# One decoder step on one core: order of the recurrence's last chunks, and where the output weights lie in memory

## The chip, the cores and the metric

The kernel runs on one NeuronCore of a Trainium2 chip. The metric is the device time of one execution in microseconds (us), taken as the median of several runs. The engines are TensorE (PE; its weight loads are listed apart as PEld), VectorE (DVE), ScalarE (ACT), GpSimd (POOL) and SyncE (SP, which here only issues DMAs). DMAs are issued by SP and by POOL; each of the two has one queue of its own, which it works through in order.

## The reference

One inference step of a two-layer decoder in float32, for a prompt of 16 + 1024 rows and eight samples of 8 rows each. Layer one is an mLSTM with 8 heads (key width 64, value width 128); layer two is an attention layer. Each is followed by a SwiGLU network. The part that matters here, for one layer-one chunk:

```python
s = jnp.einsum('bhtk,bhsk->bhts', q, k) * jnp.exp(dmat - m_t[..., None])
num = w_inter[..., None] * jnp.einsum('bhtk,bhkv->bhtv', q, C) + jnp.einsum('bhts,bhsv->bhtv', s, v)
h = num / jnp.maximum(jnp.abs(den), jnp.exp(-m_t))[..., None]
C_new = w_c[..., None, None] * C + jnp.einsum('bhs,bhsk,bhsv->bhkv', w_g, k, v)
...
h = rmsnorm(h.transpose(0, 2, 1, 3), mh_g)
out = (h.reshape(B, T, HV).astype(xn.dtype) * jax.nn.sigmoid(og)) @ w_out
```

The outputs are the rows of both groups, the new states, and the keys and values.

## The kernel before

Activations lie with the model dimension on the partitions (8 blocks of 128) and the 1104 rows (80 sample and meta rows, 1024 prompt rows) along the free dimension. A product in nearly full precision is made of three matmuls: each operand is split into a high part (a copy that rounds to the matmul's type, on ACT) and a low part (the difference, by a subtraction), and high x high, low x high and high x low are added up in PSUM (`mm3`, lines 206 to 208).

`recurrence` goes through nine chunks: chunk 0 of 80 rows, chunks 1 to 8 of 128. For a chunk, `chunk_load` fetches queries and keys (qk), decay rows (eb) and query weights (wb) through POOL's queue; `chunk_decay` makes eight DVE operations on eb and ACT takes its exponential; `chunk_scores` multiplies keys by queries (PE, sps) and the result by eb (DVE); `chunk_keys` prepares kw and wb (DVE); `chunk_state` makes the new state C (PE cp, DVE, then POOL multiplies C by the chunk's decay); `chunk_out` makes the outputs in two halves z = 0 and 1, each from a carried product (PE nps from C and wb) and an intra-chunk product (PE nps from vA and eb), which DVE (den) and ACT (vA) take out of PSUM. All of this is written out by hand in program order (`manual_schedule` for PE, DVE, ACT and POOL), a chunk ahead where it can be.

Between these steps PE gets other work by the calls `f(n)` and `g(n)`. Up to chunk 6 both issue n slices of the output gate's projection (mmA, 24 matmuls a tile): ACT takes a finished tile out with a sigmoid (stg, line 994) and POOL stores it in memory (ogD). Three chunks make a group of rows; once a group is done, `norm_heads` normalises it in two steps: five small DVE operations and a square root on ACT (fA, line 1606), then, from DVE, the three multiplications of vA. For chunks 7 and 8 `g` issues gated heads instead, one a call whatever n is: `gate_head` transposes a head on PE into a PSUM bank (ghps, line 1628), multiplies it by gain and gate values on DVE (line 1629) in the place that holds these values (ogqk, ogeb), and splits it into xh (ACT, line 284) and xl (DVE, line 285). mmA and ghps share two PSUM banks. A place is filled again by a DMA through POOL's queue (line 1010). Ten heads are gated within the recurrence and fourteen later.

Then `mlp` starts with the output projection: units of 24 matmuls (pops), one per column group t (0 to 3, 276 rows each) and weight block m (0 to 7), each added to the hidden rows H by DVE. Its weights wait in memory, split already, as eight pairs of 1.05 MB (woD); SP loads them at line 547. Pairs 0 to 3 go to four tiles of a new pool (wo) that takes over memory of the recurrence, pairs 4 to 7 to slots that the recurrence's last tiles free. A load waits until what lay at its place is finished.

## Time and profile before

| | us |
|---|---|
| median of 3 runs | 2790.65 (2790.15 to 2793.41) |
| profiled execution, whole | 2792.57 |
| profiled execution, span | 2790.8 |
| PE busy | 2730.0 (98%) |
| DVE busy | 1786.6 (64%) |
| ACT busy | 1167.3 (42%) |
| POOL busy | 847.1 (30%) |

The recurrence ends and the output units begin near 410 us of the span. In rows of the profile a name such as `ghps<-ident,vA` is output and inputs by the program's tile names; L1628 is line 1628 of the kernel; a bracket at the end of a row gives the idle time of that engine before the instruction and what ended it. Rows with several instructions (x8) are merged, and their time is the sum.

### The profile page before, as it was taken

The numbers are of one execution on the slowest core, as the hardware profiler recorded it, in microseconds if no ns is written. First come the engines' busy times: TensorE is split into PE (matmuls) and PEld (weight loads), VectorE is DVE, ScalarE is ACT, GpSimd is POOL, SyncE is SP. The second block draws the span as 40 slices with busy tenths as digits, with TensorE's granted clock in tenths as the row PEclk, the third lists the DMA queues.
The fourth block names the chain that finished last, engine by engine and source line by source line (L and its number), as shares of the span: only waits on it lengthen the run. The fifth ranks groups of instructions, "written<-read, shape, count | busy, mean of one in ns | idle before, by whom it ended". The sixth has DMA issues, their size and how long they took to land. (4 is left out here: it accounts for less than half of the span.)

```text
span 2790.8 us, 60492 instructions
## 1 busy us (share of the span) xinstructions
PE 2730.0 (98%) x23525; PEld 2637.2 (94%) x23525; DVE 1786.6 (64%) x4008; ACT 1167.3 (42%) x2291; POOL 847.1 (30%) x1305
## 2 busy tenths in 40 slices
PE   9999989999999999999999999999999999999998
PEld 8999979999999999999999998777999999999998
DVE  5633556888887665573455444777388888765656
ACT  5432552423322333443444555777343223323345
POOL 3142333132322332124353202454313223323211
PEclk9999999999999999999999999999999999999999
DMA  7667556355554375544553786443524555526556
GB/s 213 178 182 180 153 153 207 100 151 167 166 174 146 114 240 177 194 148 153 187 178 129 239 292 201 162 138 95 150 82 132 177 176 167 163 91 229 185 193 222
DMA packets 432466, 473.06 MB, mean 170 GB/s; under 512 B 37015, under 2 KB 358291, under 8 KB 431155
## 3 DMA queue, kind: packets, MB, share of 16 engines
q1 hardware_dynamic: 380690, 320.25, 37.6%
q0 software_dynamic: 44848, 142.74, 15.6%
q10 hardware_dynamic: 6640, 6.21, 0.7%
q8 instruction: 185, 3.03, 0.4%
q14 instruction: 103, 0.84, 0.1%
HBM read 322.24 MB, written 146.83 MB: 168 GB/s over the span
## 5 line engine op out<-in xcount | busy, mean ns | idle before, releaser
L1685 PE MATMUL m<-xh,slot 128*128 128x276 f32 (+1 forms) x2752 | 538.9, 289 | 1.8 <-ACT fs L1714 1.8
L1685 PEld LDWEIGHTS m<-xh,slot 128*128 128x128 f32 x2752 | 439.0, 188 | 4.2 <-ACT fs L1714 2.4
L1685 PE MATMUL m<-xl,slot 128*128 128x276 f32 (+1 forms) x1376 | 396.7, 288 | 0.0
L1685 PEld LDWEIGHTS m<-xl,slot 128*128 128x128 f32 x1376 | 259.0, 188 | 0.0
L206 PE MATMUL tmps<-slot,xh 128*128 128x256 f32 (+2 forms) x864 | 243.2, 281 | 0.0
L208 PE MATMUL tmps<-slot,xl 128*128 128x256 f32 (+2 forms) x864 | 240.6, 278 | 0.0
L207 PE MATMUL tmps<-slot,xh 128*128 128x256 f32 (+2 forms) x864 | 240.6, 278 | 0.0
L285 DVE TENSOR_TENSOR slot<-slot,slot 128x1024 fp32r<-128x1024 f32 x124 | 162.0, 1307 | 60.7 <-ACT slot L284 59.2
L284 ACT CAST slot<-slot 128x1024 fp32r<-128x1024 f32 x124 | 129.4, 1044 | 143.2 <-PE m L1685 109.4
L207 PEld LDWEIGHTS tmps<-slot,xh 128*128 128x128 f32 (+1 forms) x864 | 159.2, 184 | 0.1
L206 PEld LDWEIGHTS tmps<-slot,xh 128*128 128x128 f32 (+1 forms) x864 | 158.4, 183 | 0.3
L208 PEld LDWEIGHTS tmps<-slot,xl 128*128 128x128 f32 (+1 forms) x864 | 158.6, 184 | 0.0
L206 PE MATMUL mmA<-xh,whi 128*128 128x384 f32 (+1 forms) x384 | 134.2, 349 | 3.1 <-ACT stg L994 3.0
L207 PE MATMUL mmA<-xl,whi 128*128 128x384 f32 (+1 forms) x384 | 128.1, 334 | 0.0
L208 PE MATMUL mmA<-xh,wlo 128*128 128x384 f32 (+1 forms) x384 | 128.0, 333 | 0.0
L285 DVE TENSOR_TENSOR slot<-vA,slot 128x1024 fp32r<-128x1024 f32 (+1 forms) x59 | 82.2, 1396 | 32.7 <-ACT slot L284 31.5
L285 DVE TENSOR_TENSOR slot<-Ht,slot 128x1024 fp32r<-128x1024 f32 (+1 forms) x59 | 82.1, 1395 | 32.7 <-ACT slot L284 31.5
L284 ACT CAST slot<-vA 128x1024 fp32r<-128x1024 f32 (+1 forms) x59 | 60.8, 1035 | 95.5 <-PE m L1685 90.5
L1789 DVE TENSOR_TENSOR ws<-ws 128x128 f32<-128x128 f32 x264 | 94.7, 359 | 8.9
L284 ACT CAST slot<-Ht 128x1024 fp32r<-128x1024 f32 (+1 forms) x59 | 60.7, 1034 | 94.6 <-PE m L1685 84.1
L2919 ACT ACTIVATE s<-s,nb 128x272 f32<-128x272 f32 (+7 forms) x126 | 98.9, 787 | 0.0
L2954 ACT COPY th<-tp 128x768 f32<-128x768 f32 (+1 forms) x80 | 73.5, 921 | 56.0 <-PE tp L2946 32.2
(793 smaller groups left out, 8631.7 us busy)
## 6 DMA issues: line engine op xcount, KB each, us to landing
ws<-in_w_down SPq DMA_DIRECT2D x176, 128.0 KB, 2.7
sD<-ws SPq DMA_DIRECT2D x176, 128.0 KB, 2.1
slot<-sD SPq DMA_DIRECT2D x40, 512.0 KB, 4.2
slot<-in_w_gate_up SPq DMA_DIRECT2D x36, 512.0 KB, 4.1
kp<-in_cache_k SPq DMA_DIRECT2D x32, 512.0 KB, 5.3
vp<-in_cache_v SPq DMA_DIRECT2D x32, 512.0 KB, 7.3
vA<-in_w_gate_up SPq DMA_DIRECT2D x26, 512.0 KB, 4.0
Ht<-in_w_gate_up SPq DMA_DIRECT2D x26, 512.0 KB, 4.0
```

The source lines that it names most:

```text
L206: mm(ps, sh, mh, start=first, stop=False)
L207: mm(ps, sh, ml, start=False, stop=False)
L208: mm(ps, sl, mh, start=False, stop=last)
L284: self.nc.scalar.copy(hi, src)
L285: self.nc.vector.tensor_tensor(out=lo, in0=src, in1=hi.bitcast(F32), op=ALU.subtract)
L1685: nc.tensor.matmul(u.ps[h, b], w[p][:, k], x[q][:, k], start=first and k == i == 0, stop=k == 3 and i == 2, skip_group_check=True)
L1789: tt(out=o, in0=a, in1=b, op=ALU.subtract)
L2919: nc.scalar.activation(ss[z, u], ss[z, u], AF.Exp, bias=nb[:, z : z + 1], accum_out=sm[:, u, z : z + 1])
L2954: nc.scalar.copy(th.rearrange("p x z (u h q) -> p h (x z u) q", h=2, q=64)[:, :, :n], pt[:, :, :n])
```

## The change

Five edits, none of which changes what is computed:

- **norm first.** Behind a chunk's first half, norm's first step is issued ahead of the eight decay operations.
- **loads half a chunk sooner.** The loads for chunk i + 3, which stood at the start of chunk i + 1, are issued right behind chunk i's second half.
- **heads one at a place.** In chunks 7 and 8 the five heads stand at five places: ahead of the state, behind it, behind the first half, within the second half, and behind it, instead of three and two in a row.
- **xl on POOL.** The ten heads within the recurrence subtract xl on POOL instead of DVE. The fourteen later ones keep DVE.
- **output weights.** The wo pool is shifted by a pad of 768 bytes a partition, and pairs 1 and 2 take other tiles of it. Pair 3 is loaded twice: a first copy into a tile of its own (wo3), which unit (0, 3) reads, and a second one behind pairs 4 to 7 into the pool's lowest tile, which column groups 1 to 3 read. The tile pool TA is opened after column group 0 instead of before.

On DVE, in chunk 6 (rd and fA are norm's small steps, eb the decay operations, den and vA the copies and the normalised rows). Before:

```order
L1419 TENSOR_TENSOR wb_4487<-qk_4485,wb_4487 128x512
L1381 SCALAR_TENSOR_TENSOR eb_4486<-eb_4486,tmA,cap 128x128 x8
L1601 SCALAR_TENSOR_TENSOR rd_4562<-den 128x24
L1602 TENSOR_TENSOR rd_4562<-rd_4562,tmA 128x24
L1603 RECIPROCAL rd_4562<-rd_4562 128x24
L1604 TENSOR_TENSOR fA_4563<-ssqA,rd_4562 128x24
L1605 TENSOR_TENSOR fA_4563<-fA_4563,rd_4562 128x24
L1608 RECIPROCAL fA_4563<-fA_4563 128x24
```

And of the change:

```order
L1442 TENSOR_TENSOR wb_4299<-qk_4298,wb_4299 128x512
L1628 SCALAR_TENSOR_TENSOR rd_4554<-den 128x24
L1629 TENSOR_TENSOR rd_4554<-rd_4554,tmA 128x24
L1630 RECIPROCAL rd_4554<-rd_4554 128x24
L1631 TENSOR_TENSOR fA_4555<-ssqA,rd_4554 128x24
L1632 TENSOR_TENSOR fA_4555<-fA_4555,rd_4554 128x24
L1404 SCALAR_TENSOR_TENSOR eb_4453<-eb_4453,tmA,cap 128x128 x8
L1635 RECIPROCAL fA_4555<-fA_4555 128x24
L1636 TENSOR_TENSOR fA_4555<-fA_4555,rd_4554 128x24
```

Norm's five small steps have moved ahead of the eight decay operations; the rest of the step, which waits for ACT's square root, stands behind them.

On POOL, from the last two gate stores of the recurrence before chunk 7's state to the load of the hidden rows (C is the state, ogqk and ogeb the places of gate values). Before:

```order
L1010 DMA ogeb_4648<-ogD 128x336 x2
L1455 TENSOR_TENSOR C_107<-C_106,wcP 128x516
L1010 DMA ogqk_4647<-ogD 128x336 x2
L1010 DMA ogeb_4648<-ogD 128x336 x2
L1010 DMA ogqk_4782<-ogD 128x384 x2
L1302 DMA out_p_C<-C_105 64x4x128 x2
L995 DMA ogD<-stg_4820 128x384
L506 DMA vA<-hD 128x8x276
```

And of the change, up to the places' last refill:

```order
L1021 DMA ogeb_4648<-ogD 128x336 x2
L1660 TENSOR_TENSOR xl<-ogqk_4647,xh 128x336
L1478 TENSOR_TENSOR C_107<-C_106,wcP 128x516
L1660 TENSOR_TENSOR xl<-ogqk_4647,xh 128x336
L1021 DMA ogqk_4647<-ogD 128x336
L1660 TENSOR_TENSOR xl<-ogeb_4648,xh 128x336
L1021 DMA ogqk_4647<-ogD 128x336
L1660 TENSOR_TENSOR xl<-ogeb_4648,xh 128x336
L1021 DMA ogeb_4648<-ogD 128x336
L1660 TENSOR_TENSOR xl<-ogqk_4647,xh 128x336
L1021 DMA ogeb_4648<-ogD 128x336
L1021 DMA ogqk_4782<-ogD 128x384 x2
```

A subtraction now stands ahead of the state's multiplication, and one between every two refills, so that a refill waits in the queue for the subtractions ahead of it.

On PE, in chunk 7, from the state to the intra-chunk product of the second half. Before:

```order
L1448 MATMUL cp_4686<-vA,kw_4338 64x129 x4
...
L1415 MATMUL kps_4707<-ident,qk_4485 128x128 x4
L1628 MATMUL ghps_4714<-ident,vA 128x80
L1628 MATMUL ghps_4714<-ident,vA 128x128 x2
L1628 MATMUL ghps_4721<-ident,vA 128x80
L1628 MATMUL ghps_4721<-ident,vA 128x128 x2
L1628 MATMUL ghps_4729<-ident,vA 128x80
L1628 MATMUL ghps_4729<-ident,vA 128x128 x2
L1521 MATMUL nps_4736<-vA,eb_4335 128x129 x2
```

And of the change:

```order
L1655 MATMUL ghps_4680<-ident,vA 128x80
L1655 MATMUL ghps_4680<-ident,vA 128x128 x2
L1471 MATMUL cp_4687<-vA,kw_4300 64x129 x4
L1471 MATMUL cp_4693<-vA,kw_4300 64x129 x4
L1655 MATMUL ghps_4700<-ident,vA 128x80
L1655 MATMUL ghps_4700<-ident,vA 128x128 x2
...
L1438 MATMUL kps_4721<-ident,qk_4452 128x128 x4
L1655 MATMUL ghps_4729<-ident,vA 128x80
L1655 MATMUL ghps_4729<-ident,vA 128x128 x2
L1544 MATMUL nps_4736<-vA,eb_4297 128x129 x2
```

Two of the three heads that stood in a row behind the keys have moved to either side of the state product (cp). The diff:

```diff
--- before.py
+++ after.py
@@ -534,17 +534,24 @@
                 load = lambda e, t: self.load_h(e, H, t)
                 cut = lambda a: a[:, : KT * P].rearrange("p (k n) -> p k n", k=KT)
                 ws = []
-                for _ in range(4):
+                for x in range(4):
+                    if heads and x == 1:
+                        wp.tile([P, 192], F32, name="wopad")
                     w2 = wp.tile([P, 2, KT, P], F32R, name=self.uid("wo2"))
                     ws.append((w2[:, 0], w2[:, 1]))
                 held = [(cut(slots[a]), cut(slots[b])) for a, b in (
                     ((2, 6), (3, 7), (4, 8), (5, 9)) if heads else ((4, 5), (8, 9), (2, 6), (3, 7)))]
-                ws = [ws[x] for x in (3, 2, 1, 0)] + held if heads else held + ws
+                ws = [ws[x] for x in (3, 1, 2, 0)] + held if heads else held + ws
                 raws_open = ExitStack()
+                again = None
                 if heads:
-                    for m in range(KT):
+                    rp = raws_open.enter_context(self.pool(self.uid("wo3"), side="right"))
+                    again = rp.tile([P, 2, KT, P], F32R, name=self.uid("wo3"))
+                    rp.tile([P, 4248], F32, name="wo3pad")
+                    again = again[:, 0], again[:, 1]
+                    for m, to in [(m, again if m == 3 else ws[m]) for m in range(KT)] + [(3, ws[3])]:
                         for z in range(2):
-                            nc.sync.dma_start(ws[m][z].bitcast(F32), self.woD[m][:, z])
+                            nc.sync.dma_start(to[z].bitcast(F32), self.woD[m][:, z])
                 else:
                     rp = raws_open.enter_context(self.pool(self.uid("woraw"), side="right"))
                     rs = [rp.tile([P, KT, P], F32, name=self.uid("woraw")) for _ in range(6)]
@@ -555,8 +562,9 @@
                         if m in (4, 6, 7):
                             for t in (0,) if m == 4 else (1,) if m == 6 else (2, 3):
                                 load(nc.sync, t)
-                raws_open.close()
-                TA = self.turned(turned.enter_context(self.pool(self.uid("TA"), side="right")), f"{l}A")
+                if not heads:
+                    raws_open.close()
+                    TA = self.turned(turned.enter_context(self.pool(self.uid("TA"), side="right")), f"{l}A")
 
                 def unit(t, m, x):
                     ps = pp.tile([P, 512], F32, name=self.uid("pops"), tag="po")
@@ -566,7 +574,7 @@
                         for i, (a, b, k) in enumerate(seq):
                             nc.tensor.matmul(ps[:, :SL], a[:, k], b[:, k], start=i == 0, stop=i == len(seq) - 1)
                     else:
-                        self.fm_cols(ps[:, :SL], *ws[m], self.X[t])
+                        self.fm_cols(ps[:, :SL], *(again if again and (t, m) == (0, 3) else ws[m]), self.X[t])
                     nc.vector.tensor_tensor(out=H[t][:, m], in0=H[t][:, m], in1=ps[:, :SL], op=ALU.add)
                     self.add_sq(H, t, m, sp, x, KT - 1 if t < 2 else KT - 3)
                     if t % 2:
@@ -596,6 +604,9 @@
                         while gate(1):
                             pass
                         load(nc.gpsimd, 1)
+                if heads:
+                    raws_open.close()
+                    TA = self.turned(turned.enter_context(self.pool(self.uid("TA"), side="right")), f"{l}A")
                 fixed.close()
                 order.enter_context(self.tc.manual_schedule(engines={E.PE, E.DVE, E.Activation}))
                 weights.load(0)
@@ -1018,7 +1029,7 @@
                 if t < 0:
                     return False
                 og = ready.pop(0)
-                self.gate_head(t, left[t].pop(0), v, og, pp, tag)
+                self.gate_head(t, left[t].pop(0), v, og, pp, tag, not callable(op))
                 if not callable(op):
 
                     used.append(og)
@@ -1240,15 +1251,20 @@
             g, norm = f, iter(())
             places, state = [], None
             gate = gate(places)
+            N2 = load(3)
             for i in range(1, NT):
-                N2 = load(i + 2) if i + 2 < NT else None
+                N3 = None
                 if i + 1 < NT:
                     f(12 if i == 1 else 3)
                     self.chunk_scores(i + 1, N, rp, *args, None)
 
                 def between():
                     nonlocal state
+                    if i > 6:
+                        g(1)
                     self.chunk_state(i, R, *args, wcP, g)
+                    if i > 6:
+                        g(1)
                     if i == NT - 1:
                         state = self.last_state(C[i % 2], pp, rp)
                         next(state)
@@ -1258,16 +1274,23 @@
                 def after():
                     if i + 1 < NT:
                         self.chunk_keys(i + 1, N, pp, tm)
+                    next(norm, None)
                     if N2:
                         self.chunk_decay(i + 2, N2, tm, cap)
+                    g(2)
+                    if i < 7:
+                        g(3)
+                        g(2)
                     next(norm, None)
-                    g(2)
-                    g(3)
-                    g(2)
-                    next(norm, None)
+
+                def done():
+                    nonlocal N3
+                    if i + 3 < NT:
+                        N3 = load(i + 3)
 
                 self.chunk_out(i, R, rp, *args, den, ssq, g, exp=N2 and (lambda: N2["exp"]()),
-                               then=(lambda: next(state, None)) if i == NT - 1 else None, between=between, after=after)
+                               then=(lambda: next(state, None)) if i == NT - 1 else None, between=between, after=after, done=done,
+                               amid=(lambda: g(3)) if i > 6 else None)
                 for _ in norm:
                     pass
                 norm = self.norm_heads(i // 3, v, rp) if i % 3 == 2 else iter(())
@@ -1286,7 +1309,7 @@
                         if i == NT - 1:
                             f(2)
                         gate(0) or gate(1)
-                R, N = N, N2
+                R, N, N2 = N, N2, N3
             f(1000)
             order.close()
             for _ in norm:
@@ -1457,7 +1480,7 @@
 
 
 @_add(Net)
-def chunk_out(self, i, R, rp, pp, kp, C, v, qkD, eD, wD, tm, den, ssq, f, sp=None, exp=None, then=None, between=None, after=None):
+def chunk_out(self, i, R, rp, pp, kp, C, v, qkD, eD, wD, tm, den, ssq, f, sp=None, exp=None, then=None, between=None, after=None, done=None, amid=None):
 
     nc = self.nc
     L = TT[i][1] - TT[i][0]
@@ -1466,7 +1489,7 @@
     W = 96
     nps = []
 
-    def done(ps, g, hs):
+    def leave(ps, g, hs):
 
         hx = slice(hs[0], hs[0] + 3, 2)
         nc.vector.tensor_copy(den[:L, i, hx], ps[:L, :, DV])
@@ -1504,7 +1527,7 @@
                 f(1)
                 for j in range(4):
                     nc.tensor.matmul(o, qm[:, j * T0 : (j + 1) * T0], R["C0"][:, j, h, :], start=False, stop=(j == 3))
-            done(ps, g, hs)
+            leave(ps, g, hs)
     else:
 
         ps = None
@@ -1521,13 +1544,17 @@
                     nc.tensor.matmul(ps[a][:L, x, :], at[:L, h, :L], v(i)[:L, h, :], start=(z == 1 and x == 0),
                                      stop=(z == 0 and x == 1), skip_group_check=True)
             if z:
+                if amid:
+                    amid()
                 carried(ps, False)
             for a in range(2):
-                done(ps[a], 2 * z + a, (4 * z + a, 4 * z + 2 + a))
+                leave(ps[a], 2 * z + a, (4 * z + a, 4 * z + 2 + a))
             if z == 0:
                 after()
+        done()
         f(2)
-        f(2)
+        if i < 7:
+            f(2)
     if exp:
         exp()
     if then:
@@ -1616,7 +1643,7 @@
 
 
 @_add(Net)
-def gate_head(self, t, h, v, og, pp, tag):
+def gate_head(self, t, h, v, og, pp, tag, ahead):
 
     nc = self.nc
     yh, yl = self.xs
@@ -1628,7 +1655,9 @@
         nc.tensor.transpose(ps[:, t0 - g0 : t1 - g0], v(i)[: t1 - t0, h, :DV], self.ident[: t1 - t0, : t1 - t0])
     nc.vector.scalar_tensor_tensor(out=og[:, :n], in0=ps[:, :n], scalar=self.gain[:, G_MH + h : G_MH + h + 1],
                                    in1=og[:, :n], op0=ALU.mult, op1=ALU.mult)
-    self.split(og[:, :n], yh[:, h, g0:g1], yl[:, h, g0:g1])
+    hi, lo = yh[:, h, g0:g1], yl[:, h, g0:g1]
+    nc.scalar.copy(hi, og[:, :n])
+    (nc.gpsimd if ahead else nc.vector).tensor_tensor(out=lo, in0=og[:, :n], in1=hi.bitcast(F32), op=ALU.subtract)
 
 
 @_add(Net)
```

## The prediction

> **What bounds the kernel now.** I read the page's engine rows first, then the waits of TensorE (PE) between 250 and 460 us, then its busy time in 10 us stretches, then the instructions in order of time.
>
> ```profile
> PE 2730.0 (98%) x23525; PEld 2637.2 (94%) x23525; DVE 1786.6 (64%) x4008; ACT 1167.3 (42%) x2291; POOL 847.1 (30%) x1305
> ...
> PE ghps L1628 <- DVE ogqk L1629: 3.8, 3, 1.7
> PE mmA L206 <- ACT stg L994: 3.0, 2, 2.1
> PE pops L208 <- DMA wo<-woD: 2.3, 2, 2.1
> PE ghps L1628 <- ACT stg L994: 1.4, 1, 1.4
> PE ghps L1628 <- DVE ogeb L1629: 1.0, 2, 0.7
> ...
> 380.00:390.00 10.00, 7.85 (x61) 7.27 (x61) 6.09 (x12) 7.77 (x24) 3.42 (x7) 0.83 0.34 109
> 390.00:400.00 10.00, 6.72 (x46) 5.40 (x44) 5.36 (x13) 3.13 (x8) 2.58 (x4) 0.83 0.19 52
> 400.00:410.00 10.00, 7.03 (x67) 5.60 (x66) 6.02 (x21) 5.60 (x17) 4.34 (x7) 1.00 0.70 212
> 410.00:420.00 10.00, 7.44 (x57) 6.97 (x56) 7.98 (x26) 4.99 (x15) 2.17 (x4) 1.00 0.91 291
> 420.00:430.00 10.00, 9.31 (x72) 9.10 (x73) 6.19 (x11) 3.17 (x7) 3.42 (x5) 1.00 1.03 406
> ```
>
> PE is busy 98% of the span: only its idle time, 60.8 us in all, can be won. The change adds and removes no matmul. Its places lie where PE stands still: 380 to 421 us, the last two chunks of the recurrence and the first output units (pops), where 420 to 430 is nearly full again. A stretch row gives its length, the busy time of PE, its weight loads, DVE, ACT and POOL, the granted clock, the DMA engines' share and GB/s. The clock is twice only 0.83, so the stalls cost more than they last.
>
> **First place: norm's first step.**
>
> ```profile
> 338.12 0.44 PE L206 MATMUL mmA<-xh,whi 128*128 128x384 f32 x1 [0.87 <-ACT stg L994]
> ...
> 376.69 2.19 DVE L1381 SCALAR_TENSOR_TENSOR eb<-eb,tmA,cap 128x128 f32<-128x128 f32 x8 [1.76 <-DMA eb<-eD]
> 380.06 0.31 ACT L1606 ACTIVATE fA<-fA,eps 128x24 f32<-128x24 f32 x1 [4.99 <-DVE fA L1605]
> 381.69 0.45 ACT L994 ACTIVATE stg<-mmA 128x336 f32<-128x336 f32 x1
> 382.19 0.69 PE L206 MATMUL mmA<-xh,whi 128*128 128x384 f32 x1 [2.15 <-ACT stg L994]
> ...
> 385.54 0.34 PE L207 MATMUL mmA<-xl,whi 128*128 128x384 f32 x1
> 385.72 0.34 PE L208 MATMUL mmA<-xh,wlo 128*128 128x384 f32 x1
> ```
>
> DVE runs eight decay steps, which themselves wait 1.76 for the late load of eb, before norm's five small steps. ACT therefore waits 4.99 for its square root, and behind it stands the gate product stg that must empty a PSUM bank for PE. Norm's step before the decays removes 2.19 + 1.76 = 3.95 from ACT's start: stg would run at 381.69 - 3.95 = 377.74, and PE wants the bank at 382.19 - 2.15 = 380.04, so 2.3 is spare. The decays, now 1.2 later behind norm, do not wait for eb any more: its load is issued when chunk i's last carried product ends, not behind the gate store that follows it. The 2.15 goes. What goes with it is slow clock: from 382.19 to 385.54 PE issued ten matmuls, against 0.18 each at the end of the rows; 3.35 - 1.8 = 1.5. The same chain cost 0.87 at 338.12. Term: 2.15 + 1.5 + 0.87 = 4.5 (low end 2.2, if the clock still falls or the 0.87 has another cause; nothing below, since ACT keeps its other work).
>
> The earlier loads move nothing else onto PE: POOL now waits for PE before it issues three loads, and a gate store queued behind them is about 1 us later; the store has three stg buffers ahead of it. I cost that at nothing (with the buffers gone, up to 1 us a chunk for five chunks).
>
> **Second place: one gated head at a place.**
>
> ```profile
> 387.77 1.29 DVE L1400 TENSOR_TENSOR eb<-sps,eb 128x512 f32<-128x512 f32 x2 [3.18 <-ACT jk L1542]
> 392.38 0.68 DVE L1419 TENSOR_TENSOR wb<-qk,wb 128x512 f32<-128x512 f32 x1
> 393.69 0.48 PE L1628 MATMUL ghps<-ident,vA 80*128 80x80 f32 x3 [1.66 <-DVE ogqk L1629]
> 394.08 0.51 DVE L285 TENSOR_TENSOR xl<-ogqk,xh 128x336 fp32r<-128x336 f32 x1 [0.54 <-ACT xh L284]
> 394.50 0.56 DVE L1629 SCALAR_TENSOR_TENSOR ogqk<-ghps,gain,ogqk 128x336 f32<-128x336 f32 x1
> 395.47 1.66 PE L1521 MATMUL nps<-vA,eb 128*128 128x129 f32 x8
> 397.06 1.23 PE L1488 MATMUL nps<-C,wb 64*128 64x129 f32 x8
> 400.79 1.10 PE L1448 MATMUL cp<-vA,kw 128*64 128x129 f32 x16
> 407.26 1.05 PE L1521 MATMUL nps<-vA,eb 128*128 128x129 f32 x8
> 408.25 0.71 PE L1488 MATMUL nps<-C,wb 64*128 64x129 f32 x8
> ```
>
> A head's bank comes free after its transposes (0.48) and the gating on DVE (0.56), and DVE first did the previous head's xl. Heads back to back pay the three rows of ghps in the waits above, 3.8 + 1.4 + 1.0 = 6.2 of idle; and the products at 395.47 and 397.06 took 1.66 and 1.23 where the same ones at 407.26 and 408.25 took 1.05 and 0.71: 1.1 more lost to the clock, 7.3 together.
>
> With xl on POOL the cycle is 0.48 + 0.56 and hand-offs, about 1.15. Between two heads now stands a product of 0.7 (carried), 1.05 (intra-chunk) or 1.10 (state), plus the heads' own 0.35, so the bank is mostly free in time. What I expect to remain is walked by hand in the new order, each instruction behind the one before it on its engine and behind what releases it, at the durations of the rows here: head 2 waits 0.4, since DVE multiplies two score tiles first (1.29); head 4 waits 0.7, behind a key and a query product (0.68 each); head 5 waits 0.2; chunk 8's first carried product waits 0.7 and its second intra-chunk one 0.8, because ACT now casts a head before it empties their banks; head 7 and 8 0.1 each. Together 3.0, an estimate from these rows; 1.5 if DVE's work hides more, 6 if each hand-off is late by 0.4. No gap is long enough for me to expect the low clock again. Term: 7.3 - 3.0 = 4.3 (1.3 to 5.8).
>
> POOL's part of it has no row before, so I bound it by POOL's and the refills' nearest rows.
>
> ```profile
> L2997 POOL TENSOR_TENSOR xl<-og,xh 128x256 fp32r<-128x256 f32 x32 | 24.3, 758 | 2.6
> 358.01 1.89 POOL L1455 TENSOR_TENSOR C<-C,wcP 128x516 f32<-128x516 f32 x1 [1.42 <-DVE C L1452]
> 389.88 1.05 POOL L1455 TENSOR_TENSOR C<-C,wcP 128x516 f32<-128x516 f32 x1 [3.55 <-DVE C L1452]
> ```
>
> Between 758 ns for 256 columns and 1.05 us for 516 stand 336 columns: 0.85, against DVE's 0.51. Ten of these make 8.5 us in some 17, which POOL has (2.58 and 4.34 busy in 10). xl is first read by output unit 0, and its last needed head is subtracted about 2 us before: hidden. The same shape costs 1.05 or 1.89; at the dear end a subtraction takes 1.5.
>
> By the Trainium skill ("SBUF — State Buffer", section "SBUF: two separate sides") a DVE operation with two SBUF inputs and a POOL operation that reads SBUF exclude each other. The 1.89 ran beside DVE's wlo subtraction from SBUF, so this trace agrees; by the rule one query product (wb) would wait for xl and head 4 stand 0.85 longer, and the sum be 0.85 less.
>
> **Third place: the output weights.**
>
> ```profile
> SPq L547 <- DMA ogD<-stg: 7.9, 1, 7.9
> ...
> 410.23 0.38 PE L206 MATMUL pops<-xh,wo 128*128 128x276 f32 x1
> ...
> 414.52 0.39 PE L206 MATMUL pops<-xh,wo 128*128 128x276 f32 x1 [0.98 <-DVE noP L1309]
> 420.49 0.39 PE L208 MATMUL pops<-xh,wo 128*128 128x276 f32 x1 [2.06 <-DMA wo<-woD]
> 424.33 0.39 PE L208 MATMUL pops<-xh,wo 128*128 128x276 f32 x1 [0.20 <-DMA wo<-woD]
> ```
>
> Pair 2's memory overlaps the last gate product's stg, so SP's queue waited 7.9 for that store, and pair 3 behind it came 2.06 late. In the new order pair 1 waits for the gate store before the last one, pair 2 and the first copy of pair 3 only for the last mmA matmuls, which end near 395 in my walk. With 3.3 a unit (414.52 - 0.98 - 410.23) and the units beginning near 401, pairs 2 and 3 have some 12 to 16 us. The 2.06 and the 0.20 go. The 0.98 goes too: noP stood behind two heads' xl on DVE, which are now on POOL. Term: 3.2 (low end 1.0, if one weight load stays late).
>
> The second copy of pair 3 is 1.05 MB, behind the eight slot loads; it is first read eleven units on, some 35 us after unit 0 begins. At the 406 GB/s of the busiest stretch it takes 2.6 us of transfers: hidden, 2.6 if not.
>
> **Sum.** 4.5 + 4.3 + 3.2 = 12.0 against the profiled span, 2790.8 us: 2778.8. That execution took 2792.57, 1.8 outside the span; the median of the runs is 2790.65, so my forecast for a median is 2778.6. All best ends give 13.5 (2777.2), all low ends 4.5 (2786.2).
>
> **Rivals.**
>
> *Late refills, half the gain.* A head's gate values come back into its place by a DMA that POOL issues behind the subtraction.
>
> ```profile
> vA<-hD POOLq DMA_DIRECT2D x2, 1104.0 KB, 8.3
> ogqk<-ogD POOLq DMA_DIRECT2D x4, 168.0 KB, 2.6
> ogc<-ogD POOLq DMA_DIRECT2D x11, 192.0 KB, 6.5
> DMA to landing us min/median/max: 2.9/5.2/13.8
> ```
>
> Head 5 needs the refill behind head 2's subtraction, head 8 that behind head 5's: two landings in a row on the path, with 2.0 between (gating 0.56, a cast near 0.5, subtraction 0.85). PE's own way from head 2's subtraction to the units is 11 us in my walk; less that 2.0 and 1.1 behind head 8's landing, each may take 4.0, and at 2.6 both are covered. They now fly while pairs 2 and 3 load. At ogc's 6.5 the loss is 2 x 2.5 = 5: 2783.6. For it: pairs 2 and 3 start just then. Against: ogc's 6.5 stood behind the 1.1 MB of vA on its own queue, and these refills do not.
>
> The skill ("DMA: Bandwidth & Descriptors", section "Queues, rings and completion order") has each DMA engine alternate between queues packet by packet; by that a refill beside one other queue takes about twice its transfer, 0.4 more at the 406 GB/s, and the cover holds. No run here shows it yet.
>
> *Given back in the output units.* From 420 to 430 the DMA engines are full (share 1.03). If slot loads, hidden rows and gate rows land no earlier than they did, PE stands at unit 4 until its old time and all 12.0 is gone: 2790.6, no change. Against it: pairs 2 and 3 leave this stretch, and the slot loads wait for DVE and ACT work that also comes earlier.
>
> *Slower.* The refill loop again, at wo's longest landing, 13.8 (the last row, for the output weights): two landings exceed the cover by 2 x 9.8 = 19.6, 7.6 more than the sum: 2798. It turns to a loss from 10.0 a refill. Only a queue that serves the weights wholly first would do it.
>
> **Chances and range.** Forecast 0.68; late refills 0.15; given back 0.12; slower 0.05. A measurement of this kernel tells some 0.2% from no change, 5.6 us: faster means below 2785.1. The forecast and most late-refill cases lie there: 0.81; same 0.14; slower 0.05. The range reaches below the best ends by some 2 of issue time that I may not see (2775.0), and above to the late refills and the sum of the low ends (2786.0); it leaves out the two last rivals.
>
> **What would show it.** Right: no idle before mmA for stg at 338 and 380; granted clock 1.00 from 380 to 400; pops begin near 401 and run with no wait for wo; heads' waits together under 4. Wrong: DVE's gating released by ogqk or ogeb transfers; PE waiting for slot or for vA at pops; ACT's casts holding the PSUM copies for more than 1 us each; the same idle at 380, because something other than norm holds ACT.

## The result, and the profile after

The changed kernel takes 2780.97 us (median; 2778.11 to 2784.39) against 2789.77 of the kernel before in the same comparison: a ratio of 0.9967, 95% interval 0.9957 to 0.9978, so 8.8 us or 0.33% faster. Its profiled execution spans 2780.1 us against 2790.8. The forecast was 2778.6 (2775.0 to 2786.0).

Two places of the program serve as marks, since among the fourteen profiles here the time ahead of the first mark differs by up to 3.1 us and the long tail by up to 3.5: the transposes `nnp` behind the sampled sums, and the first output unit (`pops`). A third mark is the second norm product (L398), which stands among the units of the third column group. Between them stand these rows of the stretches of the kernel before (length, PE busy, weight loads, DVE, ACT, POOL, granted clock, DMA share, GB/s; first `nnp` to `pops`, then `pops` to L398):

```profile
284.21:410.23 126.02, 116.76 (x945) 107.78 (x946) 68.64 (x183) 68.37 (x187) 47.53 (x67) 0.97 0.51 143
410.23:479.82 69.59, 66.24 (x527) 65.26 (x525) 41.87 (x88) 22.99 (x54) 26.16 (x40) 1.00 0.71 243
```

and of the changed kernel:

```profile
283.46:400.48 117.02, 113.29 (x946) 105.62 (x946) 68.18 (x176) 68.39 (x187) 52.93 (x74) 1.00 0.59 163
400.48:469.43 68.95, 66.27 (x527) 65.22 (x525) 40.82 (x85) 22.93 (x53) 30.20 (x44) 1.00 0.74 246
```

The recurrence gave 9.00, the output units only 0.64. Idle of PE (length less busy) fell from 9.26 to 3.73 in the first and from 3.35 to 2.68 in the second. The other 3.5 of the first stage is busy time, 116.76 against 113.29, for the same matmuls; 3.31 of it is time lost at half clock.

The changed kernel's 10 us stretches and PE's waits from 250 to 460:

```profile
380.00:390.00 10.00, 9.22 (x93) 7.91 (x92) 6.22 (x15) 6.17 (x24) 6.25 (x9) 1.00 0.65 213
390.00:400.00 10.00, 7.05 (x66) 5.79 (x65) 7.66 (x18) 6.32 (x19) 7.97 (x13) 1.00 0.78 228
400.00:410.00 10.00, 10.00 (x83) 9.91 (x80) 7.70 (x23) 4.90 (x15) 5.96 (x8) 1.00 0.96 313
410.00:420.00 10.00, 9.41 (x74) 8.96 (x74) 6.29 (x12) 3.60 (x8) 4.75 (x7) 1.00 0.96 338
420.00:430.00 10.00, 9.79 (x79) 9.57 (x78) 4.48 (x8) 2.42 (x5) 4.31 (x6) 1.00 1.07 365
...
440.00:450.00 10.00, 8.61 (x67) 8.31 (x67) 8.29 (x15) 3.98 (x8) 6.16 (x9) 1.00 0.69 219
...
PE nps L1544 <- ACT vA L1503: 1.9, 1, 1.9
PE nps L398 <- DVE sq L390: 1.4, 1, 1.4
PE ghps L1655 <- DVE ogqk L1656: 0.8, 1, 0.8
PE ghps L1655 <- DVE ogeb L1656: 0.7, 1, 0.7
PE pops L208 <- DMA slot<-woD: 0.7, 2, 0.5
PE nps L378 <- ACT sq L356: 0.5, 1, 0.5
```

The waits for stg, wo and noP are gone, the clock is 1.00 in every stretch shown, and the units begin at 400.48. New are a wait of 1.9 before an intra-chunk product of chunk 8, and 2.6 in the units (slot 0.7, sq 0.5 and 1.4) where the kernel before had 3.3 (wo 2.3, noP 1.0).

The 1.9 in order of time, with what runs on POOL, DVE and ACT ahead of it:

```profile
395.70 0.90 POOL L1660 TENSOR_TENSOR xl<-ogqk,xh 128x336 fp32r<-128x336 f32 x1
396.55 0.90 POOL L1660 TENSOR_TENSOR xl<-ogeb,xh 128x336 fp32r<-128x336 f32 x1
395.45 2.03 DVE L1327 COPY nnP<-C 128x4 f32<-128x4 f32 x1
397.40 0.21 DVE L1495 COPY den<-nps 128x2 f32<-128x2 f32 x2
397.58 0.65 ACT L1503 COPY vA<-nps 128x256 f32<-128x256 f32 x2 [1.53 <-DVE den L1495]
398.00 1.16 PE L1544 MATMUL nps<-vA,eb 128*128 128x129 f32 x8 [1.89 <-ACT vA L1503]
```

The same copy of four columns in the kernel before:

```profile
404.14 0.17 DVE L1304 COPY nnP<-C 128x4 f32<-128x4 f32 x1
```

It now takes 2.03 instead of 0.17 and ends with the second of two POOL subtractions. Behind it on DVE stands den, behind den on ACT the copy that empties PE's bank.

In the units, DVE and then PE:

```profile
420.55 0.62 DVE L1656 SCALAR_TENSOR_TENSOR ogc<-ghps,gain,ogc 128x384 f32<-128x384 f32 x1 [2.38 <-DMA ogc<-ogD]
430.55 0.62 DVE L1656 SCALAR_TENSOR_TENSOR ogc<-ghps,gain,ogc 128x384 f32<-128x384 f32 x1 [3.59 <-DMA ogc<-ogD]
436.95 0.44 DVE L578 TENSOR_TENSOR vA<-vA,pops 128x276 f32<-128x276 f32 x1 [2.63 <-DMA vA<-hD]
442.49 0.70 PE L398 MATMUL nps<-sq,ones 92*128 92x276 f32 x2 [1.40 <-DVE sq L390]
```

In the kernel before, the waits that answer to the last two DMA rows were 1.78 and 1.08, and PE did not wait for sq there:

```profile
440.87 0.62 DVE L1629 SCALAR_TENSOR_TENSOR ogc<-ghps,gain,ogc 128x384 f32<-128x384 f32 x1 [1.78 <-DMA ogc<-ogD]
445.72 0.44 DVE L570 TENSOR_TENSOR vA<-vA,pops 128x276 f32<-128x276 f32 x1 [1.08 <-DMA vA<-hD]
```

### The profile page after: what moved, and what is told of

It is laid out like the page before. It is cut to its first block, busy times and chain, and to the rows that moved or that the text cites. A ratio compares the mean times of both kernels' runs of the same rounds, so it can differ in the third digit from the quotient of the medians.

```text
span 2780.1 us, 60501 instructions
## 1 busy us (share of the span) xinstructions
PE 2723.8 (98%) x23525; PEld 2632.1 (95%) x23525; DVE 1785.5 (64%) x3998; ACT 1167.7 (42%) x2291; POOL 858.1 (31%) x1315
```

## The experiments

Twelve runs follow, eleven of other kernels and one of the changed kernel again, each also timed against the kernel before (its median was 2789.6 to 2790.6 in these comparisons). The table splits both stages of every profile in the same way: idle is length less PE's busy time, slow is half of PE's busy time in the stretches at half clock. What is left is the work, 112.8 to 113.7 in the recurrence and 65.3 to 66.5 in the units in all fourteen profiles.

| kernel | nnp to pops: length, idle, slow | pops to L398: length, idle, slow | median us | ratio to before (95%) |
|---|---|---|---|---|
| before | 126.0, 9.3, 3.3 | 69.6, 3.4, 0 | 2789.77 | 1 |
| norm first alone | 119.6, 6.3, 0 | 69.9, 3.4, 0 | 2782.97 | 0.9978 (0.9968 to 0.9988) |
| norm first and loads | 120.8, 4.8, 3.1 | 68.8, 2.8, 0 | 2782.65 | 0.9974 (0.9964 to 0.9983) |
| changed, xl on DVE | 119.5, 5.8, 0 | 69.5, 2.1, 1.7 | 2784.74 | 0.9983 (0.9974 to 0.9993) |
| changed, old places | 125.1, 7.8, 4.5 | 70.0, 1.9, 2.7 | 2787.26 | 0.9994 (0.9984 to 1.0004) |
| changed, old weights | 118.7, 3.7, 1.7 | 67.3, 1.6, 0 | 2780.33 | 0.9963 (0.9949 to 0.9978) |
| changed | 117.0, 3.7, 0 | 69.0, 2.7, 0 | 2780.97 | 0.9967 (0.9957 to 0.9978) |
| changed, again | 117.0, 3.7, 0 | 69.9, 2.4, 1.7 | 2781.32 | 0.9969 (0.9958 to 0.9980) |
| second copy later | 118.6, 3.7, 1.7 | 68.8, 3.1, 0 | 2783.57 | 0.9981 (0.9971 to 0.9990) |
| nnP on ScalarE | 117.4, 4.1, 0 | 68.7, 1.4, 1.7 | 2782.01 | 0.9970 (0.9959 to 0.9981) |
| refill at once | 117.2, 3.9, 0 | 67.7, 1.6, 0 | 2779.34 | 0.9962 (0.9948 to 0.9976) |
| refill and nnP | 115.9, 2.7, 0 | 68.6, 2.3, 0 | 2780.61 | 0.9969 (0.9957 to 0.9982) |
| and the norm later | 117.4, 1.3, 3.4 | 66.7, 1.2, 0 | 2779.94 | 0.9963 (0.9951 to 0.9976) |
| and old weights | 116.3, 1.6, 1.7 | 71.1, 2.8, 2.9 | 2781.60 | 0.9967 (0.9956 to 0.9979) |

Medians a few us apart are not told apart by these intervals. The idle of the recurrence is: four profiles of the same recurrence (changed, changed again, old weights, second copy later) all have 3.73. That of the units is less firm: the changed kernel's two profiles have 2.68 and 2.41, made up of other waits (see the last run).

**Norm first alone**, in the kernel before:

```diff
-                    if N2:
-                        self.chunk_decay(i + 2, N2, tm, cap)
                     next(norm, None)
+                    if N2:
+                        self.chunk_decay(i + 2, N2, tm, cap)
```

> The kernel before with one of the five edits: norm's first step ahead of the decays; the loads stay where they were. Prediction's theory (norm's place gives 2.15 and 0.87; the loads of half a chunk sooner only cover the decays that now stand behind norm, with eb 1.76 late): PE's waits for stg are gone or under 0.6 together, idle from nnp to the first unit falls from 9.3 to 6.0 to 6.8 (4.8 with both edits). Rival (the loads are what counts, since the decays wait for eb and hold DVE): waits for stg of 1.5 us or more stay.

```profile
283.67:403.26 119.59, 113.30 (x946) 105.34 (x946) 68.07 (x183) 68.27 (x187) 47.53 (x67) 1.00 0.54 150
```

Idle falls from 9.26 to 6.29, by 2.97; PE waits for stg before no mmA matmul, though one head still waits 1.4 for it, as before. ACT's waits for its square root (fA) fall from 8.6 in two to 2.1. The prediction's theory holds, and the loads are not needed for it. The loads do what was said of them all the same: in the recurrence DVE's decays waited 5.0 for eb's loads before, 2.4 here, and not at all in the next run and in the changed kernel. By the medians this one edit brings 0.22% (0.12 to 0.32%) where all five bring 0.33%. In its profile both half clock stretches of the recurrence (3.31) are gone, though the heads stand where they did.

**Norm first and the loads half a chunk sooner**, in the kernel before (norm's lines as above; `load(i + 3)` behind the last carried product instead of `load(i + 2)` at the chunk's head):

> The kernel before with two of the five edits: norm's first step ahead of the decays, and the loads of a chunk half a chunk sooner. Prediction's theory: PE's waits for stg (3.0 us in two) are gone, 380 to 390 has a granted clock of 1.00, the units begin 4.5 us sooner than 410.23, at 405.7 (405.2 to 406.5); the heads' and weights' waits stay as before. Rival (norm is not what holds ScalarE there, the heads' places or xl on POOL took the stall away in the changed kernel): the wait of 2.15 stays and the units begin after 408.5. For the span: 2786.3 if nothing is given back behind it; 2790.8 if the units take all back.

The units begin at 405.89. One stretch held PE busy for 1.68 of 3.41 us; the two behind it ran at half clock:

```profile
388.80:392.21 3.41, 1.68 (x14) 1.47 (x14) 2.33 (x6) 0.94 (x2) 0.58 (x1) 1.00 0.05 13
392.21:395.63 3.42, 2.76 (x16) 1.79 (x15) 1.66 (x6) 1.59 (x4) 1.07 (x2) 0.50 0.42 127
395.63:399.04 3.41, 3.41 (x27) 2.67 (x25) 2.77 (x12) 1.98 (x9) 1.59 (x3) 0.50 0.43 128
```

The stall is gone as predicted. What the loads add can't be read: idle is 1.5 less than with norm first alone, but 3.08 of slow clock stand in its place, and a slow PE waits less.

**xl back on DVE**, in the changed kernel:

```diff
-    (nc.gpsimd if ahead else nc.vector).tensor_tensor(out=lo, in0=og[:, :n], in1=hi.bitcast(F32), op=ALU.subtract)
+    nc.vector.tensor_tensor(out=lo, in0=og[:, :n], in1=hi.bitcast(F32), op=ALU.subtract)
```

> The changed kernel with the ten subtractions xl of the recurrence back on DVE; the heads keep their new places. Prediction's theory (POOL is needed: DVE's xl stands between a head's transposes and the next gating): with 0.51 of DVE per head and none on POOL, the heads' waits grow by 1 to 3 us, the units begin at 401.5 to 403.5. Rival (the new places alone win the heads' idle, and the subtractions on POOL lock DVE out): the waits for ogqk, ogeb and vA, 3.7 us together in the changed kernel, fall to 2 or less, the units begin at 398.5 to 400, nnP<-C is back at 0.2 and the odd squares of chunk 7 at 0.3 each. noP stands behind two heads again, so up to 1.0 comes back in front of unit 1 under both.

```profile
399.45 0.51 DVE L1660 TENSOR_TENSOR xl<-ogqk,xh 128x336 fp32r<-128x336 f32 x1 [1.56 <-ACT xh L1659]
402.07 0.37 DVE L1327 COPY nnP<-C 128x4 f32<-128x4 f32 x1
402.93 1.16 PE L1544 MATMUL nps<-vA,eb 128*128 128x129 f32 x8 [3.20 <-ACT vA L1503]
```

The copy is short again (0.37), yet the same product waits 3.20 instead of 1.89: DVE now stands behind ScalarE's cast before each subtraction, and den behind that. The stage is 2.5 longer, 0.46 of it a wait for wo. The heads themselves wait less than in the changed kernel (0.5 against 1.5), against what was expected; the products behind them wait more. POOL is needed, and the rival falls.

**The heads in their old places**, three and two in a row, xl on POOL:

```diff
-                    if i > 6:
-                        g(1)
                     self.chunk_state(i, R, *args, wcP, g)
-                    if i > 6:
-                        g(1)
...
-                    if i < 7:
-                        g(3)
-                        g(2)
+                    g(3)
+                    g(2)
...
-                               amid=(lambda: g(3)) if i > 6 else None)
+                               amid=None)
...
-        if i < 7:
-            f(2)
+        f(2)
```

> The changed kernel with the heads of the last two chunks back in their old places, three and two in a row; their subtractions stay on POOL. Prediction's theory (a head's bank needs transposes, gating and hand-offs, about 1.15 us, and only a product between heads hides it): every head behind another waits 0.6 to 1.3, PE's waits for ghps rise from 1.5 to 4 to 6, and the units begin 119 to 121 us behind nnp instead of 117.0. Rival (the subtraction on POOL frees DVE enough, the places add nothing): 117.0 give or take 0.8, with ghps waits of 2.5 or less.

The heads' waits are 4.2, as the theory said, but the stage is 125.1, where 119 to 121 was expected. Of that, 3.65 is a side effect: the first weight pair's load waited in SP's queue for a head's transposes (43.2 us, PE ghps) and was issued at 401.16. Another 4.5 is clock:

```profile
386.20:389.61 3.41, 1.63 (x14) 1.18 (x13) 2.16 (x6) 1.22 (x3) 0.22 (x2) 1.00 0.01 3
389.61:393.02 3.41, 2.87 (x15) 2.64 (x17) 1.06 (x2) 0.94 (x2) 2.99 (x5) 0.50 0.12 20
...
PE pops L206 <- DMA wo<-woD: 3.6, 1, 3.6
```

Without these two it is 116.9, with 4.1 of idle against 3.7. In the changed kernel the heads wait 2.7 less, but products wait 2.2 that do not wait here: in the old places the copy nnP takes its 0.17, with xl on POOL, since no subtraction runs beside it. So, as far as this run tells, the new places hardly shorten the idle; they spread it, and half clock follows where it is crowded. How much they win by themselves stays open, since a PE at half clock waits less. Why the first pair's memory then hangs on a head was not followed.

**The copy nnP on ScalarE:**

```diff
-    nc.vector.tensor_copy(n, C[:, :, DV])
+    nc.scalar.copy(n, C[:, :, DV])
```

> The changed kernel, with one instruction moved: the 4-column copy nnP<-C of the last state goes from DVE to ScalarE. In the changed kernel it took 2.03 us on DVE (0.17 before) beside two xl subtractions on POOL, and PE then stood 1.89 us before the second intra-chunk product of chunk 8. Port theory (POOL's subtractions lock DVE out where DVE reads and writes SBUF only): the wait of 1.89 falls under 0.4, the output units begin 1.4 to 1.9 us sooner than 400.45, so near 398.8, and the span falls by at most that (2778.2 to 2778.8), less what the full DMA engines behind it take back. Rival, late refills: DVE's queue is held by the gate refills and ScalarE's casts, the copy only stands in it; then 1 us or more of idle stays in front of the same product, and the units begin after 399.8.

```profile
401.44 0.57 DVE L1656 SCALAR_TENSOR_TENSOR ogeb<-ghps,gain,ogeb 128x336 f32<-128x336 f32 x1 [3.85 <-DMA ogeb<-ogD]
402.06 0.55 PE L1655 MATMUL ghps<-ident,vA 128*128 128x128 f32 x3 [1.90 <-DVE ogeb L1656]
```

The copy takes 0.19, the wait of 1.89 falls to 0.35, and nothing is won: head 10 now waits 1.90 for head 8's bank, because head 8's gate values land late. Each theory is right in one half. Whether the refill had stood hidden beside the copy all along is what the next two runs ask.

**The refill at once**, and then **both**:

```diff
-                    if len(used) > 1:
-                        op.append(used.pop(0))
+                    op.append(used.pop(0))
```

> The changed kernel, but a head's place is refilled directly behind its own subtraction, not one head later. Measured from the transposes of the sampled sums (nnp, 283.46 in the changed kernel) to the first output unit (400.48), which leaves the start of the program out: 117.0 us. Theory (two stalls lie side by side: DVE's 2.03 us copy behind POOL's subtractions, and the late refill of ogeb behind it, which alone held PE 1.90 us once the copy had gone): the copy still holds PE 1.9 us, DVE's wait of 1.52 for ogeb goes, and the units begin where they did, 117.0 give or take 0.5. Rival (the refills alone are the cause, the copy is long only because its engine queue stood): 1.5 us or more is won, 115.5 or less. A stretch of 3.41 us at half clock, which has come after stretches that held PE busy for 1.68 us or less, may add 1.7 to either; the granted clock tells it apart.

> Both at once: the refill behind its own subtraction and the copy nnP<-C on ScalarE. Theory of two stalls side by side: the 1.89 in front of the second intra-chunk product and the 1.90 in front of head 7 are both gone, PE's waits between 386 and 402 fall from 3.7 to 2 or less, and the units begin 115.0 us behind nnp (114.5 to 115.7), 2.0 sooner than in the changed kernel; no stretch of 3.41 us holds 1.7 of idle, so no half clock. The span falls by up to 2, if the full DMA engines behind do not take it back (PE's wait for sq and for slot weights then grow by what was won). Rival (a third cause, ScalarE's casts or the head's bank, holds the same place): 1 us or more of idle stays there and 116.3 or more.

PE's waits in the two kernels, first the refill alone:

```profile
PE nps L1543 <- ACT vA L1502: 1.6, 1, 1.6
```

and both edits:

```profile
PE ghps L1654 <- DVE ogqk L1655: 1.1, 1, 1.1
PE ghps L1654 <- DVE ogeb L1655: 0.9, 1, 0.9
PE nps L378 <- ACT sq L356: 0.9, 1, 0.9
PE nps L398 <- DVE sq L390: 0.7, 1, 0.7
```

With the refill alone DVE no longer waits for ogeb, and the copy still holds PE 1.6: 117.2. With both, both waits are gone: 115.9, idle 2.7 against 3.7. It is 1.1 and not 2.0 because the two heads that waited already (4 and 7) wait 0.45 more together and 0.35 stays in front of the product; why was not tried. The two stalls lay side by side, and removing one alone, whichever, wins nothing.

**The second copy later:**

```diff
-                    for m, to in [(m, again if m == 3 else ws[m]) for m in range(KT)] + [(3, ws[3])]:
+                    for m, to in [(m, again if m == 3 else ws[m]) for m in range(KT)]:
...
                 weights.load(0)
+                if heads:
+                    for z in range(2):
+                        nc.sync.dma_start(ws[3][z].bitcast(F32), self.woD[3][:, z])
```

> The changed kernel with the second copy of weight pair 3 (1.05 MB) issued behind the gate and up weights' first loads instead of ahead of them, so out of the stretch 400 to 425 in which the DMA engines are full. Theory (the second copy delays the gate rows and hidden rows, which delay DVE's root of the norms): DVE's waits for ogc (2.38, 1.23, 3.59) and for vA (2.63) fall by 2 to 3 us together, PE's waits for sq at 442.49 (1.40) and 433.23 (0.49) fall under 0.6 together, and the span by 1.0 to 1.5 (2778.6 to 2779.1). Rival (the stretch is full whatever stands in it, and the same waits come a little later): the span stays within 0.5 of 2780.1, or PE waits for the late copy at column group 1's unit 3, near 437, by 1 us or more.

```profile
PE nps L398 <- DVE sq L390: 1.4, 1, 1.4
PE ghps L1658 <- DVE ogc L1659: 1.2, 1, 1.2
...
395.76:399.18 3.42, 1.52 (x14) 1.28 (x14) 2.57 (x4) 1.28 (x4) 3.31 (x5) 1.00 0.90 292
399.18:402.59 3.41, 3.41 (x20) 2.85 (x19) 0.57 (x1) 0.47 (x1) 1.96 (x3) 0.50 0.96 300
```

The theory falls. The longer wait for sq stays at 1.4 and the one of 0.5 goes, but a head now waits 1.2; DVE's wait for vA goes from 2.6 to 2.9, that for ogc from 7.2 to 5.9. Up to the units the program is that of the changed kernel, with the same 3.73 of idle, yet its stage is 1.6 longer: half clock.

**The old weights**, in the changed kernel: pairs, memory and order as before, one copy of pair 3, the side memory freed ahead of the units (all lines of the diff in `mlp` taken back).

> The changed kernel without the output weights' edit: the four pairs' memory and order as before, one copy of pair 3, the side memory freed ahead of the units. From the first output unit to the second column group's norm product (469.43 in the changed kernel) PE took 68.95 us, against 69.59 in the kernel before. Prediction's theory (the edit takes 2.3 of waits for wo out of the units): those waits come back, 2 to 4 us of them since the units now begin 10 us sooner than before and the last gate store no later, and the stage takes 71 to 73. Rival (given back: the stage is bound by what the DMA engines carry, and the edit only moves which wait ends last): wo's waits come back, but those for slot (0.67) and for sq (1.40 and 0.49) go, and the stage stays between 68.5 and 70. The start of the units stays at 117.0 behind nnp, plus 1.7 with a half clock stretch.

```profile
404.52:471.85 67.33, 65.73 (x528) 65.19 (x525) 40.31 (x82) 22.39 (x52) 28.12 (x42) 1.00 0.74 252
...
PE pops L208 <- DMA wo<-woD: 1.6, 2, 1.0
```

PE waits 1.6 for wo, and not at all for slot or sq: idle 1.6 against 2.7. The stage, 67.3, is shorter than either range that was set. From nnp to L398 the two kernels take 186.04, of which 1.71 is half clock, and 185.97. The edit wins nothing here.

**The norm one unit later**, with the refill and nnP edits:

```diff
-                    if m == 0:
+                    if m == (1 if heads else 0):
                         st = self.root(0, pn)
-                    elif m == 1:
+                    elif m == (2 if heads else 1):
                         self.diag(st)
-                    elif m == 2:
+                    elif m == (3 if heads else 2):
```

> The kernel with the refill behind its own subtraction and the copy nnP<-C on ScalarE, and beside them the first column group's norm (root, diagonal, spread) one output unit later, at units 1, 2 and 3 of the second group instead of 0, 1 and 2. From the first output unit to the second norm product PE was busy or slow for 65.5 to 66.3 us in every run, and stood idle for the rest. Theory (the norm's chain on DVE is what the units wait for now: sq 0.70 and 0.87, 1.6 of the 2.3 idle): both waits go, the stage takes 67.0 instead of 68.6, nnp to that product 183.0 instead of 184.5 (186.0 in the changed kernel), and the median 2777 to 2780. Rival (the full DMA engines set the stage; the wait only moves): PE waits instead for slot weights or for the banks that DVE empties, 1.5 us or more in the units, and nnp to that product stays at 184 or more.

```profile
400.97:467.69 66.72, 65.53 (x527) 65.02 (x525) 40.45 (x85) 22.82 (x53) 29.98 (x44) 1.00 0.76 254
```

Both waits for sq are gone, and the one for slot too; one head waits 1.1 for its gate values. The units take 66.7, the shortest of all, as the theory of the norm's chain asks. It is not shown by this: the changed kernel's second profile has no wait for sq either, with nothing edited (see the last run), and the units idle for only 1.4 and 1.6 in two profiles that leave the norm where it was. From nnp to L398 it is 184.15 and not 183.0, since 6.82 us of half clock, which cost 3.41, fell into the recurrence. The median, 2779.94, is 1.4 below that of the changed kernel in the same comparison (2781.32): less than the intervals tell apart.

**The norm one unit later, with the old weights:**

> The same kernel without the output weights' edit (four pairs as before, one copy of pair 3). With the edit put back in the changed kernel the units took 67.3 instead of 68.95. Theory (the edit is worth nothing here: it takes away the waits for wo and brings a second copy, 1.05 MB, into the stretch where the DMA engines are full): PE waits 1.5 to 2.5 for wo, less for slot, and nnp to the second norm product is within 1.0 of the kernel with the edit, leaving out a half clock stretch of 1.7. Rival (the edit pays once the norm chain is out of the way): 2 us or more longer than with the edit.

The same without the weights' edit takes 187.37, 4.59 of it slow clock; without that, 182.8 against 180.7. By idle alone it is 4.4 against 2.4 and speaks for the rival; but the slow stretch at 410 itself begins behind a wait for wo (1.76) in a stretch that held PE busy for 1.66. One profile each does not settle it.

**The changed kernel again**, unedited:

> The changed kernel once more, nothing edited. Clock theory (the granted clock is halved for one stretch of a grid of 3.413 us that runs freely, whenever the stretch before held PE busy for 1.68 us or less; the first profile had 1.70 in its worst stretch and escaped): the idle from nnp to the first unit is 3.7 again, but with another phase of the grid the stage may take 118.7 instead of 117.0, with one stretch of 3.41 at 0.50; either way the length less the idle less half of the slow stretch is 113.3 give or take 0.2. Rival (the clock follows the length of a single idle gap): no half clock, 117.0 again, since the longest gap is 1.9 as before.

First the stretch with the 1.9 wait in the changed kernel's first profile, then two of its second:

```profile
394.17:397.58 3.41, 1.70 (x14) 1.46 (x14) 3.41 (x7) 1.50 (x5) 2.75 (x5) 1.00 1.00 331
397.58:401.00 3.42, 3.00 (x27) 2.69 (x28) 0.60 (x2) 1.12 (x3) 1.81 (x3) 1.00 0.95 293
```

```profile
421.74:425.16 3.42, 1.69 (x12) 1.25 (x11) 2.51 (x5) 1.02 (x2) 0.55 (x1) 1.00 1.02 404
425.16:428.57 3.41, 3.41 (x17) 3.41 (x17) 1.62 (x3) 0.94 (x2) 2.96 (x4) 0.50 1.12 341
```

The recurrence took 117.01 with 3.73 idle once more; its emptiest stretch, at 394.43, held PE busy for 1.70 again, and full clock followed. This time the half clock came in the units, where no single wait was over 1.0. The theory by single gaps falls.

PE's waits in the units are others too, with nothing edited:

```profile
PE pops L208 <- DMA slot<-woD: 1.7, 2, 1.0
PE ghps L1655 <- DVE ogc L1656: 0.7, 1, 0.7
```

PE does not wait for sq at all. DVE waits 0.6 for the loads of ogc instead of 7.2, and not for the hidden rows instead of 2.6. Which releaser ends last in the units thus changes between two executions of one kernel, and one profile of each kernel does not tell what bounds them.

## Why the prediction was right or wrong

The direction, the range and the place of the units' start (400.48, "near 401") were right; of the sum of 12.0, 8.8 came by the medians. Part of it is luck: 0.75 of the earlier start lies ahead of nnp, and the profile lost nothing to half clock in the recurrence, where two others of the same recurrence (second copy later, old weights) lost 1.71. By its terms:

**Norm first, 4.5: right.** Its idle, 2.15 + 0.87 = 3.02, was measured alone at 2.97; its clock, 1.5, is one stretch at half speed, 1.66 in the kernel before. The other stretch, which the sum gave to the heads, was gone with this edit alone. The loads cover the decays as it said; that they cost PE nothing is not contradicted, but not shown either.

**Heads, 4.3: the idle nearly right, its make-up not.** The step "Together 3.0" for what remains measured 3.6 in waits. Head 4 waited 0.68 (0.7 expected), head 7 0.80 (0.1), the first carried product 0.27 (0.7), and heads 2 and 5 not at all (0.4 and 0.2). The second intra-chunk product waited 1.89 where 0.8 was set for a cast by ScalarE; the casts were not the cause, at 0.47 each. The cause is DVE's copy nnP, which the prediction does not name, at 2.03 instead of 0.17. It takes both edits of this term together: with xl back on DVE, or with the heads in their old places, the copy is short. The rule of the Trainium skill ("SBUF — State Buffer", section "SBUF: two separate sides") was weighed, but only its part on two SBUF inputs and only against one product (wb, 0.85 at most, which measured 0.68 as before; no subtraction ran beside it). The same section names fp32 copies within SBUF as well; the trace agrees, 2.03 against 0.17. The term's clock, 1.1, was credited on "No gap is long enough for me to expect the low clock again". That step failed: it is not one gap that counts (below), and the changed program ran at half clock for 3.41 us in the recurrence in the run with the second copy later.

**Output weights, 3.2: wrong by 2.5.** The step "The 2.06 and the 0.20 go. The 0.98 goes too" was right for these waits, and wrong to count them as won. Idle in the units fell by 0.7 (0.9 in the second profile); taking the edit back cost nothing in the changed kernel. What took the gain is the rival "given back in the output units", confined to this term. In the first profile ogc and the hidden rows came no sooner relative to the units, so DVE ended the norm's chain late; in the second PE waited 1.7 for slot (0.7 in the first), which the prediction had set as a sign of being wrong. Whether the DMA engines or the norm's chain bind the units stays open.

**Late refills**, given 5 us: the step "at 2.6 both are covered" failed for one of the two. The refill for head 5 took 2.65 from issue to landing, the one for head 8 took 6.17, over the cover of 4.0; the two behind it took 7.6 and 8.2. DVE's gating waited 1.5 and 1.4 for such loads, the first sign that was set for being wrong. It cost PE nothing only because the copy held it at the same time. **Slower** did not occur.

Between the two profiles of before and after, 10.7 apart, 6.2 is idle and 3.3 is clock; 1.1 lies at the start and in the tail.

## What to carry to other kernels

A wait that an edit removes is won only if the next releaser behind it is earlier too. Two stalls at one place hide each other, so an experiment that removes one and gains nothing has not cleared it; the pair has to be tried. When work moves to POOL, list every DVE instruction that reads and writes SBUF alone beside it, down to the smallest, and ask who stands behind it. And judge idle on PE by how much of it falls close together: here 1.7 us or more within one stretch of 3.41 mostly cost another 1.7 behind it.

## What the runs showed of the hardware

**Half clock comes on a grid.** In every profile the granted clock was 0.50 for whole stretches of 3.41 us, whose edges lie on a grid with one phase per execution (before: 382.09, 385.50, 395.74, 399.16; 245.56 is 40 stretches of 3.413 before the first). From 200 to 490 us in the fourteen profiles, 25 stretches at full clock had PE busy for 1.69 us or less; each was followed by half clock. Of those with 1.70 and more, all but two were followed by full clock, among them 1.70 twice; the two exceptions, at 2.26, stay unexplained, and so does one place near 164 us where half clock follows full stretches. A half clock stretch filled by PE costs 1.7 us. So the same recurrence, with the same 3.73 of idle, took 117.0 in the changed kernel and 118.6 with the second copy later: there the grid lies 0.9 us later behind nnp, and the stretch around the same waits holds 1.52 instead of 1.70. This is part of the 6 us over which one kernel's times spread. The Trainium skill ("TensorE: Matmul & The Clock Gate", section "Part 1: The HAM clock gate (the "warmup" mystery)") states such a free-running window of 3413 ns, and the trace agrees. Its table lets the clock fall after an idle window; here it fell with PE busy for up to 1.69 of the 3.41 us, and twice for 2.26, so the measurement decides.

**POOL's subtractions hold DVE, down to a copy of four columns.** Beside two of them (0.90 each) DVE's copy of four columns took 2.03, ending with the second, and 1.77 with the refill at once; it took 0.37 with no subtraction on POOL, 0.17 in the kernel before, and 0.19 on ScalarE. DVE's squares of chunk 7 (jk, both inputs from SBUF) took 0.83 and 1.38 beside a subtraction, and 0.29 without one.
